# A planner's contention rule, a choice of slots by planned release, and silu behind the second norm's Exp, in a two-layer decoder trunk

## The chip, the cores and the metric

The program runs on one core of a Trainium2 chip. The metric is the device time of one execution in microseconds; of several runs the median counts, and one execution was recorded by the hardware profiler.

## What is computed

Two layers of a decoder trunk on one sequence of 1024 tokens with 1024 channels, all in float32. Each layer has a root-mean-square norm, one input projection, four token mixers of 256 channels, a norm of each mixer's output, an output projection added to the stream, a second norm (`h2` below), and a gated feed-forward network (FFN) added to the stream.

```python
h = rmsnorm(x, attn_norm[l])
c_q, c_kv, k_r, g_b, g_c, u_conv, u_pool, q_sw, k_sw, v_sw = split(h @ w_in[l])
groups = (mla_attention(...), short_gated_conv(...), multiscale_pool(...), swa_sink_attention(...))
mixed = concat(rms_normalised(groups)) * mix_norm[l]
x = x + mixed @ w_o[l]
h2 = rmsnorm(x, ffn_norm[l])
gate, up = split(h2 @ w_gate_up[l])          # 1024 x 2 * 2816
x = x + (silu(gate) * up) @ w_down[l]        # 2816 x 1024
```

A last norm follows the second layer.

## The kernel before

**Products.** Tokens lie along the free axis, in two halves of 512; `HALVES = (1, 0)` says that the second half is worked first. Every large product is made of three matmuls (`mm3`, L260): an operand is split into a high part, which ScalarE casts to fp32r (L280, or L285 with a norm's gain), and a low part, which VectorE makes by subtracting the high part from the operand (L283, or L286 with the gain); high times high, high times low and low times high are added up in PSUM. One matmul has a 128 x 128 weight block and 512 columns.

**Storage.** SBUF is cut into 47 slots of 128 partitions x 1024 numbers, named `u0` to `u46`. `Slots.pair` takes the slot at the head of `places`, a first-in-first-out queue, and `free_pair` puts a slot back at its tail. A new tile in a slot is not written until the last instruction on the tile that it held is through: a wait on whichever engine or transfer that was. The eight PSUM banks (`ps_mm`, `ps_s`, `ps_t`, `ps_pv` and others in the program's names) are given by the planner.

**The start of the FFN.** `out_last` makes the output projection of a token half, adds it to the stream (L1181) and squares the sum (L324). The norm's root comes from `ss2.rnorm(t)`: a matmul with ones sums the squares over the channels (L340, once for the high and once for the low part), ScalarE applies Ln (L349), Exp (L350) and Square (L351), and VectorE makes a Newton step (L352, which reads the matmul's bank last, and L355). Each token half has a root of its own. The products do not wait for the roots: h2 is used without its root, and the root is multiplied into the gate and the up part behind the products (L359, L1454). Silu (L1453, ScalarE) needs another table of functions than Ln and Exp, and a change of table is an instruction of its own (ACT_TABLE_LOAD).

**Gate and up.** The 2816 columns are 22 groups `f` of 128. Group 0 is computed in the plain form, eight products of twelve matmuls (`plain(u)` for half `u`, with `plain_gates` and `plain_acts` behind it). All others use a form with seven products per pair of halves, whose operands are sums of weight blocks and sums of token blocks. Groups 1 and 2 are begun early, among the products of group 0; groups 3 to 21 run in a loop. In the loop GpSimd makes the weight sums (L1213 to L1215, L1243) and the product of silu with the root (L1454); in groups 4 to 19 it also prepares the down-projection's weights: `dn_load` loads two slots of them (L1525), `dn_sum` adds them on GpSimd (L1532) and stores them to DRAM (L1535, the tiles `qd`). The activations' combinations are made on VectorE (L1463) and stored (L1468, the tiles `ad`).

```python
1585        plain(0)
1586        r2.append(F.ap(ss2.rnorm(HALVES[0], tag="pv")))
1587        plain_gates()
1588        combine(0)
1589        plain_acts()
1590        for w in early:
1591            w.split2()
1592        early[0].start()
1593        combine(1)
1594        r2.append(F.ap(ss2.rnorm(HALVES[1], tag="pv")))
1595        plain(1)
```

**What sets the order.** The class `Order` lists every instruction of the traced program with a cost, and schedules them on TensorE, ScalarE, VectorE, GpSimd and SyncE (whose queue issues all DMAs): forward by rank, then backward, in three passes. The order so found is imposed by dependencies without a semaphore. VectorE instructions with two SBUF operands (kind `two`) and GpSimd's TENSOR_TENSOR (kind `pool`) are taken to hinder each other: where they overlap, the VectorE one is made longer by 0.6 of the overlap, up to 1.15 of its own length, and the GpSimd one by 0.6 of it, up to 0.8 us. `scheduled_kernel` repeats this four times, hands the PSUM banks out anew by the planned times each time, and keeps the order with the shortest planned span.

Of the kernel before, what the change touches and what calls it, by code (L numbers as in the profile page):

```python
# [51 lines left out]
class Slots:  # L52
# [59 lines left out]
def trunk_kernel(ctx: ExitStack, tc: tile.TileContext, ins, out, given=None):  # L112
# [10 lines left out]
    slots = Slots(ctx.enter_context(tc.tile_pool(name="slots", bufs=1)), N_U)  # L123
# [174 lines left out]
    class SumSq:  # L298
# [35 lines left out]
        def rnorm(self, t, cols=whole, tag="t", final=None):  # L334
# [15 lines left out]
            act.activation(r0, r0, AF.Exp, scale=-0.5)  # L350
# [67 lines left out]
    for l in range(L):  # L418
# [1032 lines left out]
        def silu(g, r):  # L1451
            nonlocal last_silu
            last_silu = act.activation(g, g, AF.Silu)  # L1453
            pool.tensor_tensor(out=g, in0=g, in1=r, op=ALU.mult)  # L1454
# [123 lines left out]
        plain_acts()  # L1578
# [4 lines left out]
        r2.append(F.ap(ss2.rnorm(HALVES[1], tag="pv")))  # L1583
# [205 lines left out]
        for cols in (slice(0, 256), slice(256, HT)) if last else ():  # L1789
# [11 lines left out]
            finish(x, 1, cols)  # L1801

class Order:
# [7 lines left out]
    SHARED = 0.6  # L1813
# [114 lines left out]
    def run(self, rank, back=False):  # L1928
# [12 lines left out]
        pool = two = 0.0  # L1941
# [9 lines left out]
        for _ in range(self.n):  # L1951
            best = None
            for e in self.ENGINES:
                due(e, free[e])
                if not now[e] and not later[e]:
                    continue
                t = free[e] if now[e] else later[e][0][0]
                if e == "SP" and not back and len(flying) == self.LANES:
                    t = max(t, flying[0])
                if best is None or t < best[0]:  # L1960
                    best = t, e
            t, e = best
            due(e, t)
            k = heapq.heappop(now[e])[1]
            seen, taken = cost[k]
            order[e].append(k)
            if back:
                free[e] = t + taken
                end[k] = -free[e]
            else:  # L1970
                if kind[k] == "two":
# [229 lines left out]
```

## Time and profile before

| | before |
|---|---|
| median of 3 runs | 2063.43 us (2062.45 to 2063.79) |
| profiled execution, its time | 2062.96 us |
| its span in the trace | 2061.2 us |
| granted TensorE clock, mean | 0.998 |
| TensorE busy | 2035.3 us (99%) |
| VectorE / ScalarE / GpSimd busy | 1503.7 / 992.6 / 577.3 us |

The busy time of TensorE counts the matmuls, which are pipelined and whose ends are modelled; the weight loads beside them are listed as PEld. In the rows of the trace DVE is VectorE, ACT ScalarE, POOL GpSimd, SP or SPq the queue that issues the DMAs. A row of the timeline has the start in microseconds, the duration, the engine, the line, the operation, the tiles with their sizes, and in brackets how long the engine had idled and what ended that. A number such as "L283" is a line of the kernel's text. The first layer's FFN begins at about 390 us, the second's at about 1410 us.

### The profile page before, as it was taken

The page shows a single profiled execution, that of the slowest core. Times are in us where ns is not written, and L with a number is a line of the kernel's source. Part 1 is how long each engine was busy: PE and PEld are TensorE (multiplying, and loading weights), DVE is VectorE, ACT ScalarE, POOL GpSimd, SP SyncE. Part 2 cuts the span into 40 slices and gives each one's busy share as a digit, 9 for nine tenths or more (in the row PEclk, how much of TensorE's full clock was granted, in tenths as well). Part 3 has the DMA queues.
Part 4 walks back from the last instruction along what each step waited for, and adds up shares of the span by engine and source line. Part 5 has one row for each costly group of instructions (what it writes and reads, how often), then busy time and mean ns, then how long its engine had stood idle before and what let it go on. Part 6 is the DMA issues. An engine that isn't in the chain of part 4 may idle for free.

```text
span 2061.2 us, 26597 instructions
## 1 busy us (share of the span) xinstructions
PE 2035.3 (99%) x9422; PEld 1673.6 (81%) x9422; DVE 1503.7 (73%) x2443; ACT 992.6 (48%) x1743; POOL 577.3 (28%) x420
## 2 busy tenths in 40 slices
PE   9999999999999999999999999999999999999998
PEld 7887888778888888888888878888788877788887
DVE  8779979987666667655657898889866655585555
ACT  7447657753333334444433666668433333354342
POOL 0200000037777773000002000000577777710000
PEclk9999999999999999999999999999999999999999
DMA  5211223334554556766413112142455555487642
GB/s 191 90 57 46 84 78 96 137 133 168 181 175 167 189 169 235 265 220 208 140 46 124 37 42 97 61 144 94 159 169 178 178 175 170 154 302 237 204 171 96
DMA packets 142118, 302.37 MB, mean 147 GB/s; under 512 B 13856, under 2 KB 60960, under 8 KB 141984
## 3 DMA queue, kind: packets, MB, share of 16 engines
q1 hardware_dynamic: 141984, 300.66, 43.1%
q8 instruction: 74, 1.21, 0.2%
q14 instruction: 60, 0.49, 0.1%
HBM read 212.00 MB, written 87.56 MB: 145 GB/s over the span
## 4 chain that ended last, share of the span: by engine, by line
PE 68%; POOL 7%; DVE 5%; DMA 4%; issue 2%; ACT 2%; SPq 0%; DVEq 0%; POOLq 0%; ACTq 0%
PE ps_mm L260 25%; PE ps_s L260 21%; PE ps_t L260 8%; PE ps_pv L260 6%; POOL u L1532 3%; PE ps_pv L1044 2%; PE ps_t L1032 1%; DMA u<-in_w_dn 1%; POOL tp L1454 1%; DMA ad<-u 1%; POOL u L1214 1%; DVE u L283 1%; POOL u L1213 1%; ACT u L280 1%; DMA u<-in_w_gu 1%
## 5 line engine op out<-in xcount | busy, mean ns | idle before, releaser
L260 PE MATMUL ps_mm<-u,u 128*128 128x512 f32 (+1 forms) x3378 | 831.0, 390 | 3.4 <-ACT u L280 2.3
L260 PEld LDWEIGHTS ps_mm<-u,u 128*128 128x128 f32 x3378 | 615.4, 188 | 130.4 <-issue 5.3
L260 PE MATMUL ps_s<-u,u 128*128 128x512 f32 x2670 | 636.1, 390 | 5.8 <-DVE tn L352 2.3
L283 DVE TENSOR_TENSOR u<-u,u 128x1024 fp32r<-128x1024 f32 (+2 forms) x400 | 443.3, 1126 | 225.2 <-ACT u L280 173.4
L260 PEld LDWEIGHTS ps_s<-u,u 128*128 128x128 f32 x2670 | 499.5, 188 | 117.8 <-ACT tn L1321 3.9
L280 ACT CAST u<-u 128x1024 fp32r<-128x1024 f32 (+2 forms) x400 | 345.1, 881 | 505.4 <-POOL u L1215 60.1
L260 PE MATMUL ps_t<-u,u 128*128 128x512 f32 (+1 forms) x1124 | 255.3, 378 | 2.8 <-DVE u L1447 2.7
L260 PEld LDWEIGHTS ps_t<-u,u 128*128 128x128 f32 x1124 | 201.6, 188 | 45.8 <-DVE u L1447 6.5
L1454 POOL TENSOR_TENSOR tp<-tp,u 128x512 f32<-128x512 f32 x80 | 135.1, 1689 | 341.7 <-ACT tp L1453 341.7
L260 PE MATMUL ps_pv<-u,u 128*128 128x512 f32 x744 | 177.8, 390 | 1.6 <-DVE te L1658 1.0
L260 PEld LDWEIGHTS ps_pv<-u,u 128*128 128x128 f32 x744 | 139.3, 188 | 32.1 <-ACT tn L1321 1.9
L1041 POOL MEMSET u<- 128x128 f32 x32 | 5.9, 211 | 472.9 <-PE ps_pv L1044 149.3
L1453 ACT ACTIVATE tp<-tp 128x512 f32<-128x512 f32 x80 | 50.5, 631 | 155.2 <-DVE tp L359 155.1
L749 POOL TENSOR_TENSOR u<-u,u 128x512 f32<-128x512 f32 x4 | 6.0, 1509 | 380.4 <-PE ps_t L622 288.9
L1532 POOL TENSOR_TENSOR u<-u 128x352 f32<-128x352 f32 x64 | 80.5, 1259 | 31.6 <-DMA u<-in_w_dn 30.2
L280 ACT CAST u<-ps_t 128x512 fp32r<-128x512 f32 (+3 forms) x132 | 65.1, 504 | 48.1 <-PE ps_t L1032 26.7
L1532 POOL TENSOR_TENSOR u<-u,u 128x352 f32<-128x352 f32 x64 | 85.0, 1328 | 3.0
L285 ACT ACTIVATE u<-u,par 128x512 fp32r<-128x512 f32 x100 | 70.6, 717 | 28.5 <-DVE u L359 11.1
L283 DVE TENSOR_TENSOR u<-ps_t,u 128x512 fp32r<-128x512 f32 (+3 forms) x132 | 75.9, 582 | 11.1 <-ACT u L280 9.8
L286 DVE SCALAR_TENSOR_TENSOR u<-u,par,u 128x512 fp32r<-128x512 f32 x100 | 73.7, 750 | 5.9 <-ACT u L285 5.9
L324 ACT ACTIVATE tn<-u 128x512 f32<-128x512 f32 (+1 forms) x91 | 52.3, 595 | 48.6 <-DVE u L1723 42.1
L359 DVE TENSOR_TENSOR tp<-tp,u 128x512 f32<-128x512 f32 x76 | 72.5, 954 | 2.0
(208 smaller groups left out, 2359.3 us busy)
## 6 DMA issues: line engine op xcount, KB each, us to landing
u<-in_w_gu SPq DMA_DIRECT2D x92, 512.0 KB, 4.1
ad<-u SPq DMA_DIRECT2D x154, 256.0 KB, 3.9
u<-ad SPq DMA_DIRECT2D x70, 512.0 KB, 5.1
u<-in_w_dn SPq DMA_DIRECT2D x64, 352.0 KB, 3.4
qd<-u SPq DMA_DIRECT2D x64, 352.0 KB, 2.4
u<-qd SPq DMA_DIRECT2D x32, 512.0 KB, 4.7
u<-in_w_in SPq DMA_DIRECT2D x28, 512.0 KB, 3.5
u<-in_w_dn SPq DMA_DIRECT2D x24, 512.0 KB, 5.2
```

The lines of the kernel that those rows point to most:

```text
L260: pe.matmul(o, w, r, start=start and k == 0 and i == 0, stop=stop and k == n - 1 and i == 2, skip_group_check=again,)
L280: a = act.copy(hi, f)
L283: dve.tensor_tensor(out=lo, in0=f, in1=rd(hi), op=ALU.subtract)
L285: a = act.activation(hi, f, AF.Copy, scale=gain)
L286: dve.scalar_tensor_tensor(out=lo, in0=f, scalar=gain, in1=rd(hi), op0=ALU.mult, op1=ALU.subtract)
L324: act.activation(q, f, AF.Square)
L359: dve.tensor_tensor(out=o, in0=a, in1=b, op=ALU.mult)
L1032: pe.transpose(p[:, b * P : (b + 1) * P], pr[b][j // 4][:, (j % 4) * P : (j % 4 + 1) * P], ident,)
L1044: pe.matmul(py[:, c0:], v_of(j, h), R.ap(s)[:, c0:], start=j == 0 and n == 0, stop=j == nj - 1 and n == 1,)
L1453: last_silu = act.activation(g, g, AF.Silu)
L1454: pool.tensor_tensor(out=g, in0=g, in1=r, op=ALU.mult)
L1532: pool.tensor_tensor(out=o, in0=a, in1=b, op=ALU.add)
```

## The change

Three things are changed. First, the planner's rule for VectorE and GpSimd: instructions of the kinds `two` and `pool` that run at the same time now each get half the speed for as long as they overlap, both without a cap, apart from 0.1 us of each; in the backward pass a `pool` instruction counts 1.3 times its length. Second, `Slots.pair` takes, of the free slots, the one whose last tile is planned to be done with earliest; the planned ends come from the round before. Third, the FFN's start: `silu` of group 0 is called from `plain_acts`, `plain_acts` of the first half stands behind the second root, silu is held behind the second root's Exp by an order without a semaphore, and the second root's matmul goes to a bank of another tag. No arithmetic is added or left out: TensorE has 9394 instructions, VectorE 2445, GpSimd 425 and SyncE 860 in both programs; ScalarE has 1585 before and 1579 after, six table loads fewer.

```diff
-    def __init__(self, pool, n):
+    def __init__(self, pool, n, ends=None):
         self.pool = pool
+        self.ends = iter(ends) if ends else None
+        self.until = [0.0] * n
+        self.asked = []
         self.places = deque(range(n))
         self.halves = {F32: deque(), F32R: deque()}
         self.cur = [None] * n
         self.dt = [None] * n
     def pair(self, dt):
-        i = self.places.popleft()
+        if self.ends:
+            i = min(self.places, key=lambda p: self.until[p])
+            self.places.remove(i)
+            self.until[i] = next(self.ends)
+        else:
+            i = self.places.popleft()
         self.cur[i] = self.pool.tile([P, 2, HT], dt, name=f"u{i}", tag=f"u{i}", bufs=1)
+        self.asked.append(self.cur[i].tensor.name)
...
                 pe.matmul(p, ones, q, start=False, stop=True)
             r0, q = tmp("tn")[:, cols], tmp("tn")[:, cols]
             act.activation(r0, p, AF.Ln, scale=1.0 / n)
-            act.activation(r0, r0, AF.Exp, scale=-0.5)
+            self.exp = act.activation(r0, r0, AF.Exp, scale=-0.5)
             act.activation(q, r0, AF.Square)
             dve.scalar_tensor_tensor(
                 out=q, in0=p, scalar=-0.5 / n, in1=q, op0=ALU.mult, op1=ALU.mult
...
             for f, u, pg, pu in waiting:
                 gate = tmp("tp")
                 mul_to(gate, pg, r2[u])
-                silu(gate, r2[u])
                 gates.append((f, u, gate, pu))
             waiting.clear()
         def plain_acts():
             for f, u, gate, pu in gates:
+                silu(gate, r2[u])
                 acts[f][u] = F.half()
                 mul_to(F.ap(acts[f][u]), pu, gate)
             gates.clear()
...
         def silu(g, r):
             nonlocal last_silu
             last_silu = act.activation(g, g, AF.Silu)
+            behind(last_silu, ss2.exp)
             pool.tensor_tensor(out=g, in0=g, in1=r, op=ALU.mult)
         def combos(g):
...
         r2.append(F.ap(ss2.rnorm(HALVES[0], tag="pv")))
         plain_gates()
         combine(0)
-        plain_acts()
         for w in early:
             w.split2()
         early[0].start()
         combine(1)
-        r2.append(F.ap(ss2.rnorm(HALVES[1], tag="pv")))
+        r2.append(F.ap(ss2.rnorm(HALVES[1], tag="t")))
+        plain_acts()
         plain(1)
         early[1].start()
         combine(2)
...
-    SHARED = 0.6
+    SHARED = 1.3
+    LEAST = 0.1
...
-                if kind[k] == "two":
-                    more = min(max(0.0, min(pool, t + 2 * seen) - t) * self.SHARED, 1.15 * seen)
-                    seen, taken = seen + more, taken + more
-                    two = t + seen
-                elif kind[k] == "pool":
-                    more = min(0.8, max(0.0, two - t) * self.SHARED)
-                    seen, taken = seen + more, taken + more
-                    pool = t + seen
...
+        def on(t):
+            nonlocal clock
+            if t > clock:
+                for x in sharing.values():
+                    x[1] -= (t - clock) / len(sharing)
+                clock = t
...
+            if sharing:
+                t, e = min((clock + max(x[1], 0.0) * len(sharing), e) for e, x in sharing.items())
+                if best is None or t <= best[0]:
+                    on(t)
+                    k, _, began = sharing.pop(e)
+                    end[k] = t + self.LEAST
+                    free[e] = end[k] - cost[k][0] + cost[k][1]
+                    release(k, began)
+                    continue
...
+            if back:
+                free[e] = t + taken * (self.SHARED if kind[k] == "pool" else 1.0)
+                end[k] = -free[e]
+            elif kind[k] in ("two", "pool"):
+                on(t)
+                sharing[e] = [k, seen - self.LEAST, t]
...
+    def ends(self, end, asked):
+
+
+
+        return [max((end[k] for k in self.users[m]), default=0.0) for m in asked]
...
+        given = plan.banks(end), plan.ends(end, asked)
+        nc, traced, asked = trace(*given)
         plan = Order(traced, nc.dependency_edges)
-        found = plan.find()
-        if best is None or found[0] < best[0]:
-            best = found[0], banks, found[1]
-    return trace(best[1], best[2])[0]
+        span, order, end = plan.find()
+        if best is None or span < best[0]:
+            best = span, given, order
```

The planner's new rules change the order on all engines. Three places are shown, all in the first layer. The numbers behind a tile's name count the tiles; the slot is the number right behind `u`. A line's number after the change is 9 or 10 higher than before (L280 is L289, L283 is L292, L349 is L358, L1202 is L1211).

The first place is the second root of the FFN. ScalarE before, with Ln (L349), Exp (L350) and Square (L351) of the second root; silu of group 0 (L1453) stands further ahead:

```order
L349 ACT_TABLE_LOAD
L349 ACTIVATE tn_4232<-ps_pv_4229 128x512
L280 CAST u4_4218<-tp_4209 128x512
L350 ACT_TABLE_LOAD
L350 ACTIVATE tn_4232<-tn_4232 128x512
L280 CAST u32_4215<-tp_4210 128x512
L280 CAST u39_4222<-tp_4211 128x512
L1142 ACTIVATE te_4319<-u31_2542,par_75 128x512
L351 ACTIVATE tn_4233<-tn_4232 128x512
```

ScalarE after, with Ln (L358), Exp (L359) and Square (L360) of the same root and silu of group 0 (L1462):

```order
L358 ACTIVATE tn_4229<-ps_t_4226 128x512
L289 CAST u16_2213<-tp_4146 128x512
L359 ACTIVATE tn_4229<-tn_4229 128x512
L1462 ACT_TABLE_LOAD
L1462 ACTIVATE tp_4139<-tp_4139 128x512
L289 CAST u25_4157<-tp_4147 128x512
L1151 ACTIVATE te_4202<-u8_3957,par_75 128x512
L360 ACTIVATE tn_4230<-tn_4229 128x512
```

No table load stands among the root's steps now but the one for silu, and silu has moved behind Exp. On TensorE the root's two matmuls (L340) stood here before, among the products of group 0 and of the early groups:

```order
L260 MATMUL ps_t_4239<-u43_4069,u9_3933 128x512
L260 MATMUL ps_t_4176<-u20_3824,u33_4167 128x512 x2
L260 MATMUL ps_t_4176<-u20_3824,u46_4168 128x512
L260 MATMUL ps_t_4176<-u15_3854,u33_4167 128x512 x2
L260 MATMUL ps_t_4176<-u15_3854,u46_4168 128x512
L340 MATMUL ps_pv_4229<-u44_4076,ones_r_79 128x512 x2
L260 MATMUL ps_t_4176<-u25_3884,u33_4167 128x512 x2
```

and after the change they are L349:

```order
L269 MATMUL ps_s_4080<-u23_3914,u41_3928 128x512 x2
L269 MATMUL ps_s_4080<-u23_3914,u29_3929 128x512
L349 MATMUL ps_t_4226<-u22_4076,ones_r_79 128x512 x2
L269 MATMUL ps_s_4240<-u17_2225,u9_3932 128x512
L269 MATMUL ps_s_4172<-u39_3811,u38_3946 128x512 x2
L269 MATMUL ps_s_4172<-u39_3811,u1_3947 128x512
```

They are now TensorE's instructions 1895 and 1896; before they were 1936 and 1937. In the second layer they move by three places. The tile `u_4076` is the split sum of squares of the second half.

The second place is the beginning of group 3. VectorE before, with the addition of two products (L1658, tile `te_4670`), the weights' low parts (L283) and the combinations of the activations (L1463):

```order
L283 TENSOR_TENSOR u12_4638<-u17_4561,u22_4637 128x1024
L283 TENSOR_TENSOR u40_4620<-u6_4560,u11_4619 128x1024
L1463 TENSOR_TENSOR u35_4420<-u46_4551,u35_4420 128x512
L283 TENSOR_TENSOR u6_4673<-u27_4568,u10_4672 128x1024
L1658 TENSOR_TENSOR te_4670<-ps_pv_4587,tn_4654 128x512
```

VectorE after, where L1658 is L1668 and L1463 is L1473:

```order
L292 TENSOR_TENSOR u14_4620<-u10_4559,u2_4619 128x1024
L292 TENSOR_TENSOR u34_4638<-u38_4560,u41_4637 128x1024
L1668 TENSOR_TENSOR te_4670<-ps_pv_4587,tn_4654 128x512
L292 TENSOR_TENSOR u13_4673<-u12_4567,u11_4672 128x1024
L1680 TENSOR_TENSOR tp_4689<-ps_mm_4641,tn_4635 128x512
L1473 TENSOR_TENSOR u15_2542<-u15_2542,u33_3186 128x512
```

The addition has moved ahead of the combination and of one of the low parts. The third place is the queue of DMAs in group 9, with the loads of a later group's weights (L1202 and L1204, tiles `u_6048` and `u_6049`), the loads and stores of the down-projection's weights (L1525, L1535) and a store of activations (L1624). Before:

```order
L1202 DMA u35_6048<-in_w_gu 128x1024
L1535 DMA qd2_97<-u40_5950 128x2x352
L1535 DMA qd2_97<-u18_5949 128x2x352
L1525 DMA u31_6091<-in_w_dn 128x2x352
L1525 DMA u6_6092<-in_w_dn 128x2x352
L1204 DMA u18_6049<-in_w_gu 128x1024
L1624 DMA ad0_88<-u7_3957 128x512
L1535 DMA qd2_97<-u6_6092 128x2x352
```

After:

```order
L1211 DMA u41_6048<-in_w_gu 128x1024
L1213 DMA u34_6049<-in_w_gu 128x1024
L1545 DMA qd2_97<-u12_5950 128x2x352
L1535 DMA u24_6091<-in_w_dn 128x2x352
L1535 DMA u12_6092<-in_w_dn 128x2x352
L1634 DMA ad0_88<-u8_3957 128x512
L1545 DMA qd2_97<-u5_5949 128x2x352
L1545 DMA qd2_97<-u12_6092 128x2x352
```

The second load of the weights now stands ahead of the stores and goes to slot 34; before it went to slot 18, which the second of those stores reads. In the same way the high part of tile `u_5895` was cast into slot 40 before (`u40_6087`, the slot of the sums in `u40_5950`) and is cast into slot 26 after (`u26_6087`, the slot of a raw weight tile whose last split is earlier). From the loop's groups to the down-projection the order on TensorE itself is the same before and after; in the mixers and at the FFN's start it differs.

More of the change, by code (lines that the diff above doesn't have):

```diff
@@ L111, in trunk_kernel @@
 @with_exitstack
-def trunk_kernel(ctx: ExitStack, tc: tile.TileContext, ins, out, given=None):
+def trunk_kernel(ctx: ExitStack, tc: tile.TileContext, ins, out, given=None, ends=None):
     nc = tc.nc
@@ L1801, in trunk_kernel @@
             finish(x, 1, cols)
+    return slots.asked
 class Order:
@@ L1940, in run @@
         flying, served = deque(), 0.0
-        pool = two = 0.0
+        sharing, clock = {}, 0.0
         for k in range(self.n):
@@ L1949, in due, with release @@
                 heapq.heappush(now[e], (rank[k], k))
[L1951 to L1970, printed above, removed]
[L1971 to L1986 removed]
+        def on(t):
[4 more added lines that the diff above has]
+                clock = t
+        def release(k, t):
+            e = self.engine[k]
             for j, sync in ahead[k]:
```

62 lines of the change are left out of this document (42 added, 20 removed).

## The prediction

> **What bounds the kernel now.** I read the page first, for the engine that fills the span; then the windows of TensorE, to find in which stages it loses time; then the waits of TensorE; then the timeline around each wait. The page's row of busy times, and a table of windows (from and to, length, TensorE busy and matmuls, granted clock, DMA share, GB/s):
>
> ```profile
> PE 2035.3 (99%) x9422; PEld 1673.6 (81%) x9422; DVE 1503.7 (73%) x2443; ACT 992.6 (48%) x1743; POOL 577.3 (28%) x420
> ...
> 396.00:480.00 84.00, 79.90 (x348) 1.00 0.34 117
> 640.00:815.00 175.00, 173.09 (x756) 1.00 0.55 183
> 820.00:1010.00 190.00, 190.00 (x840) 1.00 0.67 225
> 1420.00:1500.00 80.00, 77.19 (x338) 1.00 0.37 127
> 1500.00:1640.00 140.00, 139.74 (x615) 1.00 0.51 173
> 1640.00:1830.00 190.00, 187.72 (x813) 1.00 0.55 180
> ```
>
> TensorE bounds the kernel: only 26 us of 2061.2 are not busy. The change removes no matmul, so all it can win is time in which TensorE waits or is fed late. The fourth window lies in the first layer's down-projection: 840 matmuls in 190.00 us, with no gap, 0.2262 us each. Other windows of these stages have the same kind of matmul, so what each lost is its length less its matmuls times 0.2262: 5.3 and 3.5 us in the two starts of the FFN (first and fifth window), 4.0, 0.9 and 6.1 us in the later gate and up groups (the others). That is 8.8 us and 11.0 us for the two layers together. The down-projection has nothing to win.
>
> The waits of TensorE (what waits, what for; us in total, times, longest):
>
> ```profile
> PE ps_t L260 <- DVE u L1447: 2.7, 7, 1.2
> PE ps_s L260 <- DVE tn L352: 2.3, 1, 2.3
> PE ps_mm L260 <- ACT u L280: 2.3, 2, 1.5
> ...
> PE ps_pv L260 <- DVE te L1658: 1.0, 1, 1.0
> PE ps_s L260 <- DVE te L1658: 1.0, 1, 1.0
> ...
> PE ps_pv L634 <- DVE u L283: 0.8, 1, 0.8
> PE ps_s L260 <- DVE u L1181: 0.7, 1, 0.7
> PE ps_pv L260 <- ACT tn L1321: 0.6, 1, 0.6
> ```
>
> The first row is the loop over the groups; the next four are the FFN's starts, 6.6 us of their 8.8; the last three lie in the mixers and the output projection.
>
> **The second root.** The timeline of the first layer, from the sum of squares (L326) and its low part (L283, 404.39) over the root's matmul to the product that waits for the bank:
>
> ```profile
> 399.53 0.70 DVE L326 SCALAR_TENSOR_TENSOR u<-tn,u 128x512 f32<-128x512 f32 x1
> ...
> 404.39 0.70 DVE L283 TENSOR_TENSOR u<-u,u 128x512 fp32r<-128x512 f32 x1
> ...
> 408.86 0.62 PE L340 MATMUL ps_pv<-u,ones_r 128*128 128x512 f32 x2
> ...
> 411.27 1.28 ACT L349 ACT_TABLE_LOAD   x1
> 412.56 0.60 ACT L349 ACTIVATE tn<-ps_pv 128x512 f32<-128x512 f32 x1
> ...
> 413.69 1.28 ACT L350 ACT_TABLE_LOAD   x1
> ...
> 418.61 0.68 DVE L352 SCALAR_TENSOR_TENSOR tn<-ps_pv,tn 128x512 f32<-128x512 f32 x1
> 419.35 0.97 PE L260 MATMUL ps_s<-u,u 128*128 128x512 f32 x3 [2.34 <-DVE tn L352]
> ```
>
> From the matmul's end at 409.5 to L352's end at 419.3 the chain takes 9.8 us, two table loads of 1.28 among them. After the change one load stands in it, silu's, between Exp and Square: 1.28 us less, but silu itself stands there too. What removes the stall is the place of the matmul, 41 matmuls or 41 x 0.2262 = 9.3 us earlier: the bank comes free several us ahead of its next use, and 2.3 us go.
>
> [...]
>
> The price is a new wait. Earlier by 9.3 us, the matmul comes due at 399.6. Its low part was made at 405.1, and the four low parts with a gain that stood ahead of L326 are now spread behind. L326 still has to follow the last square, and one low part with a gain and one wide low part stand between it and the tile: 399.53 + 0.70 + 0.76 + 1.24 + 0.70 = 402.9 if L326 does not gain, 400.5 if it gains the 2.4 us by which its square was done before it:
>
> ```profile
> 396.47 0.63 ACT L324 ACTIVATE tn<-u 128x512 f32<-128x512 f32 x1
> 400.73 0.76 DVE L286 SCALAR_TENSOR_TENSOR u<-u,par,u 128x512 fp32r<-128x512 f32 x1
> 401.99 1.24 DVE L283 TENSOR_TENSOR u<-u,u 128x1024 fp32r<-128x1024 f32 x1
> ```
>
> So TensorE waits 0.9 to 3.3 us here; I take 2.0, nearly the middle, and keep 0 (if other matmuls slip ahead in time as well) and 5.5 (if the tile is as late as before) for the range. In the second layer the matmul moves by three places, 0.7 us, and I count nothing.
>
> **Silu's place.** In both layers a product waited for a cast behind silu's table load:
>
> ```profile
> 426.77 1.28 ACT L1453 ACT_TABLE_LOAD   x1
> ...
> 429.68 2.56 PE L260 MATMUL ps_mm<-u,u 128*128 128x512 f32 x10 [0.73 <-ACT u L280]
> ```
>
> With all first-group silus behind the second root, Exp and silu alternate no more and this load is gone. The 2.3 us of the third wait row go in the two layers; the cast here can come 1.28 us sooner, for a wait of 0.73. Silu's product on GpSimd and the first half's activation come later, and that is free: the combinations that read them are made at group 3 (465.60 below).
>
> **The start of group 3.** Two products waited for L1658, once in each layer. VectorE and TensorE in the first:
>
> ```profile
> 465.60 1.77 DVE L1463 TENSOR_TENSOR u<-u,u 128x512 f32<-128x512 f32 x1
> 467.29 2.31 DVE L283 TENSOR_TENSOR u<-u,u 128x1024 fp32r<-128x1024 f32 x1
> 469.53 0.68 DVE L1658 TENSOR_TENSOR te<-ps_pv,tn 128x512 f32<-128x512 f32 x1
> 470.26 3.03 PE L260 MATMUL ps_pv<-u,u 128*128 128x512 f32 x12 [0.96 <-DVE te L1658]
> ```
>
> L1463 and one low part stand behind L1658 now, 4.0 us of work for a wait of 0.96. The low part that comes later is needed by a later product; I count 1.4 of the 2.0 us as won and leave 0.6 for it. The FFN's starts: 2.3 + 2.3 + 1.4 - 2.0 = 4.0 us won.
>
> **The groups.** In the loop the stall repeats in odd groups. A cast of the next group's weights, the low part behind it, L1447 behind that in VectorE's queue, and the product that wants L1447's bank:
>
> ```profile
> 644.66 1.06 ACT L280 CAST u<-u 128x1024 fp32r<-128x1024 f32 x1 [4.24 <-POOL u L1532]
> 684.07 1.05 ACT L280 CAST u<-u 128x1024 fp32r<-128x1024 f32 x1 [4.58 <-DMA qd<-u]
> 685.16 1.78 DVE L283 TENSOR_TENSOR u<-u,u 128x1024 fp32r<-128x1024 f32 x1 [2.25 <-ACT u L280]
> 685.82 2.25 POOL L1215 TENSOR_TENSOR u<-u,u 128x512 f32<-128x512 f32 x1
> ...
> 687.60 2.79 PE L260 MATMUL ps_t<-u,u 128*128 128x512 f32 x11 [1.17 <-DVE u L1447]
> ```
>
> The cast does not lack its operand. It waits for the slot it writes to: the first-in-first-out queue gave it the slot of the down-projection's sums, whose last GpSimd sum or store is late. In the new order such casts get slots of weights split long before (slot 26 instead of 40), and the loads of weights stand ahead of the stores in SyncE's queue. A cast that may start some 4 us earlier takes the low part and L1447 out of TensorE's way. What is late next: other casts now get the sums' slots, and every load that waits for a slot holds the queue behind it. Those casts have some us until their low parts are read, by the order, but their starts depend on GpSimd. So of the 11.0 us I count 6 as won; the bounds are 10, if all casts are free, and -4, if another such wait appears beside each that goes.
>
> **The mixers.** Their order changes on all engines and nothing there is aimed at a stall. The three mixer rows sum to 2.1 us. I count 1 us lost, with -2 (those waits gone) and +4 (two more sets of them) as the bounds of the cost. The four passes over weights in the down-projection keep TensorE's order: nothing.
>
> **The sum.** -6 - 4 + 1 = -9 on the profiled execution's 2062.96 us: 2053.96. The median of the runs is 0.47 above that execution, so 2054.4 us.
>
> **Rivals.** The first: the new rule is not what the chip does, so the plan's times, on which both orders and slots hang, are off by as much as the old ones.
>
> ```profile
> 440.50 2.37 DVE L283 TENSOR_TENSOR u<-u,u 128x1024 fp32r<-128x1024 f32 x1 [0.40 <-ACT u L280]
> 440.50 1.28 POOL L1213 TENSOR_TENSOR u<-u,u 128x512 f32<-128x512 f32 x1
> 446.66 1.23 DVE L283 TENSOR_TENSOR u<-u,u 128x1024 fp32r<-128x1024 f32 x1
> ```
>
> GpSimd took its 1.28 us unhindered, and VectorE took 1.23 (its time alone, third row) and 1.14 more, nearly all of GpSimd's time. Half speed each would have had both at about 2.4. So the one that is first runs through and the other stands still. [...] A VectorE step of 1.23 that meets a GpSimd step of 2.25 then ends up to 2.25 + 1.23 = 3.5 us after its start, where half speed plans 2.5: 1.0 us off, the size of the stall at 687.60. If that eats the groups' gain, the sum is 0 - 4 + 1 = -3: 2060.4 us, which is within 0.2% (4.1 us, about what a measurement of this kernel can tell from no change). Against it: the total of both steps is right by either rule, and slots, not contention, hold the casts that stall now. Chance 0.2.
>
> The second rival ends slower: slots by planned release bring the cast's wait into every group. The slot with the earliest planned end is chosen by times that assume half speed; where GpSimd's sums run later, casts and loads wait in more groups, and each waiting load holds SyncE's queue. Groups 4 to 19 of two layers are 32; 7 stall now by the first wait row, for 11.0 us, 1.6 each. With 7 more stalls and none of the old ones gone the sum is 11 - 4 + 1 = +8: 2071 us. It decides from 7 us of new stalls on, five groups, since the 3 us won elsewhere and the 4.1 us of the bound come first. For it speak 4.24 and 4.58 us of idleness before the casts above; against it, that the new order holds those waits at casts needed later. Chance 0.15.
>
> **How the numbers follow.** The forecast has 0.65. With the groups and the mixers at their good ends (-10 and -2), and no wait ahead of the root's matmul (-6), the sum is -18: 2045.4. With half of the groups' gain (-3), 5.5 us ahead of the root's matmul (-0.5) and +4 in the mixers it is +0.5, 2063.9. Neither is likely in all its parts at once. To hold eight in ten I take 2046 to 2066, which has the first rival in it and ends between it and the second. Faster by over 0.2%: nearly all of the forecast, a little of the first rival, 0.64. Within 0.2%: most of the first rival and the forecast's upper edge, 0.19. Slower: the second rival and some mishap in the mixers, 0.17.
>
> **What would show it.** Right: no table load of L358 or L359 in the FFN's start, the product behind the second root's bank not waiting, at most 3 us of waiting ahead of the root's matmul, TensorE's waits for L1456 (L1447 before) below 1.5 us in all, casts in odd groups that idle for their load and not for GpSimd or a store, and windows of the groups that lose under 5 us together. Wrong: casts that wait over 4 us for sums or stores in even groups too, a TensorE wait of 4 us or more at the second root, or more than 6 us of waits in the mixers.

## The result and the profile after

The changed kernel takes 2063.96 us (median of 13 runs, 2062.37 to 2068.96); the kernel before took 2063.78 us in the 13 runs beside it. The ratio is 1.0005, with a 95% interval of 0.9997 to 1.0014: no change that can be measured. Forecast were 2054.4 us, 0.4% faster. The profiled execution of the changed kernel took 2065.5 us, its span is 2063.7 us against 2061.2 before.

TensorE's waits in the changed kernel (line waited for, us in total, times, longest):

```profile
PE ps_t L631 <- DVE tp L620: 8.2, 8, 2.0
PE ps_t L269 <- DVE u L1456: 5.5, 6, 1.0
...
PE ps_s L269 <- DVE u L292: 1.0, 1, 1.0
PE ps_mm L269 <- ACT u L289: 0.9, 1, 0.9
```

The waits that stood at the FFN's starts are gone: none for the second root (L352 before, L361 now), none for casts where there were 2.3 (the 0.9 for L289 lies at 6.4 us, at the program's start), none for L1668 (L1658 before). Two smaller ones are new there, 1.0 for L292 in the first layer and 0.5 for L368 in the second. The first row is new and larger than all of them. L631 transposes the probabilities of the window attention, and L620 is the VectorE step that scales them. TensorE's windows after, at the places shown of before:

```profile
396.00:480.00 84.00, 82.71 (x363) 1.00 0.32 110
480.00:640.00 160.00, 158.98 (x701) 1.00 0.53 182
640.00:815.00 175.00, 173.19 (x763) 1.00 0.52 177
...
1420.00:1500.00 80.00, 79.50 (x347) 1.00 0.34 117
1500.00:1640.00 140.00, 139.11 (x614) 1.00 0.54 180
1640.00:1830.00 190.00, 188.18 (x830) 1.00 0.51 176
```

By the prediction's count (length less 0.2262 us for each matmul) the two starts lose 1.9 and 1.5 us, where they lost 5.3 and 3.5; the groups lose 1.4, 2.4, 1.1 and 2.3, 7.2 us in all against 11.0. So some 9 us were won in the FFN, where 10 were forecast, and given back in the mixers.

A second count has no windows to choose. TensorE has the same number of instructions in all the kernels here, so the start of its n-th instruction can be compared between two traces, and the difference grows or shrinks stage by stage. The stages end, in both layers alike, at the 1800th instruction of the layer (before the FFN's start), the 2400th (behind group 3) and the 3900th (in the down-projection). In us, changed less before: mixers +3.6 and +7.1, FFN's starts -2.3 and -2.1, groups -0.05 and -3.6; before rounding they sum to +2.5, the difference of the spans.

**Where the mixers lost it.** GpSimd makes sums of the early groups' weights (L758 to L761, L749 to L752 before) ahead of the FFN, in the middle of the mixers. In the kernel before, the first of them starts at 91.7 us; in the changed kernel it starts at 76.1, beside the softmax of the window attention. The timeline of the changed kernel, GpSimd, VectorE and TensorE:

```profile
76.13 1.29 POOL L758 TENSOR_TENSOR u<-u,u 128x512 f32<-128x512 f32 x1 [75.69 <-DMA u<-in_w_gu]
77.38 2.26 POOL L759 TENSOR_TENSOR u<-u,u 128x512 f32<-128x512 f32 x1
79.71 1.26 POOL L760 TENSOR_TENSOR u<-u,u 128x512 f32<-128x512 f32 x1
81.05 1.27 POOL L761 TENSOR_TENSOR u<-u 128x512 f32<-128x512 f32 x1
...
78.42 1.23 DVE L615 TENSOR_TENSOR sm<-sm,par 128x2 f32<-128x2 f32 x1
...
80.05 2.43 DVE L620 TENSOR_SCALAR tp<-tp,sm 128x256 f32<-128x256 f32 x2
...
81.27 0.30 PE L631 MATMUL ps_t<-cst,tp 128*128 128x128 f32 x1 [1.99 <-DVE tp L620]
82.53 0.78 PE L631 MATMUL ps_t<-cst,tp 128*128 128x128 f32 x3 [0.72 <-DVE tp L620]
```

The same pair of scalings in the kernel before took a quarter of that, and its two-column addition (L606 there) about a ninth; the first sums follow later. Their row merges the two sets and names, of the several transfers that they wait for, the one that landed last:

```profile
77.49 0.14 DVE L606 TENSOR_TENSOR sm<-sm,par 128x2 f32<-128x2 f32 x1
...
77.95 0.61 DVE L611 TENSOR_SCALAR tp<-tp,sm 128x256 f32<-128x256 f32 x2
...
91.75 2.72 POOL L749 TENSOR_TENSOR u<-u,u 128x512 f32<-128x512 f32 x2 [91.30 <-DMA vraw<-in_w_ukv]
```

L615 ends when the GpSimd sum beside it ends (77.38 + 2.26 = 79.64). The two scalings end shortly after one sum each (the sums at 80.97 and 82.32); the second ends at 82.48. Four such sets of sums, two in each layer, give the eight waits.

### The profile page after: what moved, and what is told of

The parts are those of the page before. It is cut to its first block, busy times and chain, and to the rows that moved or that the text cites. A ratio compares the mean times of both kernels' runs of the same rounds, so it can differ in the third digit from the quotient of the medians.

```text
span 2063.7 us, 26584 instructions
## 1 busy us (share of the span) xinstructions
PE 2033.8 (99%) x9422; PEld 1675.0 (81%) x9422; DVE 1563.2 (76%) x2443; ACT 988.9 (48%) x1737; POOL 575.6 (28%) x420
## 4 chain that ended last, share of the span: by engine, by line
PE 86%; DVE 7%; ACT 3%; issue 2%; DMA 1%; POOL 0%; SPq 0%; DVEq 0%; ACTq 0%; POOLq 0%
PE ps_mm L269 33%; PE ps_s L269 27%; PE ps_t L269 10%; PE ps_pv L269 8%; PE ps_pv L1053 2%; PE ps_t L1041 1%; DVE u L292 1%; DVE u L295 1%; PE ps_s L987 1%; PE ps_s L988 1%; PE ps_s L989 1%; DMA u<-in_w_gu 1%; ACT u L294 1%; PE ps_pv L643 1%; PE ps_t L631 1%
## 5 line engine op out<-in xcount | busy, mean ns | idle before, releaser
L292 DVE TENSOR_TENSOR u<-u,u 128x1024 fp32r<-128x1024 f32 (+2 forms) x400 | 461.0, 1173 | 185.7 <-ACT u L289 124.7
L289 ACT CAST u<-u 128x1024 fp32r<-128x1024 f32 (+2 forms) x400 | 344.9, 881 | 450.4 <-DVE u L292 81.5
L1462 ACT ACTIVATE tp<-tp 128x512 f32<-128x512 f32 x80 | 50.6, 632 | 138.4 <-DVE tp L368 138.2
L758 POOL TENSOR_TENSOR u<-u,u 128x512 f32<-128x512 f32 x4 | 6.2, 1558 | 362.7 <-DVE sm L617 271.1
L289 ACT CAST u<-ps_t 128x512 fp32r<-128x512 f32 (+3 forms) x132 | 64.9, 503 | 50.5 <-PE ps_t L1041 25.6
L1542 POOL TENSOR_TENSOR u<-u,u 128x352 f32<-128x352 f32 x64 | 82.7, 1292 | 2.1
L1542 POOL TENSOR_TENSOR u<-u 128x352 f32<-128x352 f32 x64 | 76.5, 1196 | 21.1 <-DMA u<-in_w_dn 21.1
L292 DVE TENSOR_TENSOR u<-ps_t,u 128x512 fp32r<-128x512 f32 (+3 forms) x132 | 75.5, 581 | 8.7 <-ACT u L289 7.1
L368 DVE TENSOR_TENSOR tp<-tp,u 128x512 f32<-128x512 f32 x76 | 77.6, 1021 | 1.4
```

The source lines that it names most:

```text
L289: a = act.copy(hi, f)
L292: dve.tensor_tensor(out=lo, in0=f, in1=rd(hi), op=ALU.subtract)
L368: dve.tensor_tensor(out=o, in0=a, in1=b, op=ALU.mult)
L1542: pool.tensor_tensor(out=o, in0=a, in1=b, op=ALU.add)
```

## The experiments

Port theory: the sums moved beside the softmax and hold VectorE up there, in the way of the prediction's first rival: the step that is first runs through and the other stands still. The runs can show the holding up; a port as such is visible in none of them. Order theory, its rival: the new order and slots lose time in the mixers in many places, and the sums only lie there. Stage differences are taken from each kernel's profiled execution against that of before, as above (both layers together); each ratio is to runs of the kernel before on the same chip. Plan and queue are the two ways to choose a slot:

| kernel | rule | slots | FFN's start | median, us | ratio to before, 95% interval | mixers | starts | groups |
|---|---|---|---|---|---|---|---|---|
| changed | new | plan | new | 2063.96 | 1.0005 (0.9997 to 1.0014) | +10.7 | -4.5 | -3.7 |
| a_sums_light | new | plan | new | 2054.31 | 0.9947 (0.9934 to 0.9959) | -1.0 | -4.2 | -3.4 |
| b_sums_light | old | queue | old | 2063.43 | 0.9998 (0.9989 to 1.0007) | +0.6 | +1.5 | -0.4 |
| a_dn_light | new | plan | new | 2058.33 | 0.9966 (0.9954 to 0.9979) | +5.9 | -4.5 | -11.1 |
| a_kinds | new | plan | new | 2062.09 | 0.9986 (0.9977 to 0.9994) | +9.4 | -4.5 | -3.4 |
| a_hold | new | plan | new | 2054.65 | 0.9957 (0.9943 to 0.9971) | -1.2 | -4.1 | -3.2 |
| a_fifo | new | queue | new | 2046.18 | 0.9913 (0.9900 to 0.9927) | -2.6 | -4.2 | -11.2 |
| a_fifo_hold | new | queue | new | 2046.37 | 0.9915 (0.9902 to 0.9929) | -3.1 | -1.2 | -10.9 |
| a_old_rule | old | plan | new | 2060.93 | 0.9985 (0.9976 to 0.9994) | +7.3 | -2.8 | -9.1 |
| a_old_hold | old | plan | new | 2049.91 | 0.9933 (0.9919 to 0.9946) | -1.7 | -2.9 | -8.5 |
| b_slots | old | plan | old | 2069.97 | 1.0028 (1.0015 to 1.0042) | +11.1 | +4.3 | -7.9 |
| b_rule | new | queue | old | 2050.64 | 0.9939 (0.9927 to 0.9952) | -3.4 | +1.3 | -10.2 |
| b_silu | old | queue | new | 2066.11 | 1.0009 (1.0000 to 1.0017) | -2.1 | +0.9 | +3.5 |

The changed kernel and a_dn_light have the same order in the mixers and differ there by almost 5 us in one execution each, so that column is good to some microseconds; a_dn_light's profiled execution was also the fastest of its six (2053.28). The medians carry the verdicts.

**Without the sums, in the same order.** In `a_sums_light` the plan is that of the changed kernel, and only in the program built from it (`final`) the four sums become memsets:

```diff
-            pool.tensor_tensor(out=F.ap(q + 1), in0=a21, in1=a22, op=ALU.add)
-            pool.tensor_tensor(out=F.ap(q), in0=a21, in1=a11, op=ALU.add)
-            pool.tensor_tensor(out=a21, in0=F.ap(q + 1), in1=a11, op=ALU.add)
-            pool.tensor_tensor(out=a12, in0=a12, in1=a21, op=ALU.add)
+            if final:
+                for o in (F.ap(q + 1), F.ap(q), a21, a12):
+                    pool.memset(o, 0.0)
+            else:
...
```

> The changed kernel in its own order, slots and banks, in which only the four GpSimd sums of the early groups' weights (L758 to L761, two sets in each layer) are replaced by memsets of the same tiles, so the weights of groups 1 and 2 are left out. Port theory: the mixers lose time because these sums run beside the softmax of the window attention and hold VectorE's scalings (L620) and its two-column steps (L615, L617). Then L620 falls from 455 ns to about 350, TensorE's wait for it from 8.2 us to under 1.5, and the time by 6 to 10 us, to about 2056. Order theory: the mixers' loss comes from the new order and slots in general, and the sums only happen to lie there: the waits of TensorE in the mixers stay above 5 us in all and the time falls by less than 3.

Measured: 2054.31 us, some 10 us less than the changed kernel. The group of the scalings before, in the changed kernel, and in this one (busy, mean ns of one):

```profile
L611 DVE TENSOR_SCALAR tp<-tp,sm 128x256 f32<-128x256 f32 (+1 forms) x64 | 20.0, 348 | 0.5
```

```profile
L620 DVE TENSOR_SCALAR tp<-tp,sm 128x256 f32<-128x256 f32 (+1 forms) x64 | 27.2, 455 | 0.4
```

```profile
L620 DVE TENSOR_SCALAR tp<-tp,sm 128x256 f32<-128x256 f32 (+1 forms) x64 | 19.7, 339 | 0.4
```

No wait of TensorE for L620 is left in the list; the first row is the groups' (the line numbers are 4 higher there):

```profile
PE ps_t L269 <- DVE u L1460: 5.7, 6, 1.0
```

The port theory's numbers came; the order theory's did not. Of the 11.7 us between the two kernels' mixers (+10.7 and -1.0), 8.2 are the waits for L620, and about 2 are a lower clock behind the first of them (0.91 from 80 to 100 us in the changed kernel, last section). The same memsets in the kernel before, as a control:

> The kernel before in its own order, with the same memsets in place of the same sums (the weights of groups 1 and 2 are left out). Port theory: the sums lie beside other work there (two-operand steps of the pooling mixer), so taking them away gains 0 to 2 us: 2062 to 2064. If they cost as much there as in the changed kernel (6 to 10 us), the change did not bring the loss by moving them, and the port theory falls.

Measured: 2063.43 us, a ratio of 0.9998 (0.9989 to 1.0007). Where they were, the sums cost nothing that can be measured.

**The sums held back.** `a_hold` does all the work; the two sums that stand first in each set wait by a semaphore for the scaling of the eighth attention unit, and the planner knows of it.

```diff
-            pool.tensor_tensor(out=F.ap(q + 1), in0=a21, in1=a22, op=ALU.add)
-            pool.tensor_tensor(out=F.ap(q), in0=a21, in1=a11, op=ALU.add)
+            for o, a in ((F.ap(q + 1), a22), (F.ap(q), a11)):
+                tc.add_manual_dep(
+                    pool.tensor_tensor(out=o, in0=a21, in1=a, op=ALU.add).ins,
+                    scaled[0].ins.name,
+                    mybir.DependencyInfo(mybir.DependencyClass.Sync, mybir.DependencyReason.DATA),
+                    reason="hold",
+                )
```

> The changed kernel in which GpSimd's sums for the early groups may start only when VectorE has done the scaling (L620) of the eighth unit of the window attention, by a semaphore; the planner knows of it and plans anew; all work is done. Port theory: from there to the ninth unit there is no scaling, so L620 averages under 370 ns, TensorE waits under 1.5 us for it, and the 10 us that the memsets gave come back nearly whole: 2054 to 2058. Order theory: with another order and the sums later, slots are freed later and loads queue: 2060 to 2066.

Measured: 2054.65 us. The scalings (L621 here) are back at their own length:

```profile
L621 DVE TENSOR_SCALAR tp<-tp,sm 128x256 f32<-128x256 f32 (+1 forms) x64 | 19.4, 338 | 0.2
```

Two other plans got the same semaphore: one whose sums lie late anyway (a control), and one with the old rule, whose sums lie early.

> New rule, first-in-first-out slots, silu's new place, and the semaphore that keeps the early groups' sums behind the eighth unit's scaling. A control for the semaphore: in this kernel without it the sums lie behind that scaling anyway (92 to 102 us). Port theory: the semaphore finds nothing to mend, 2044 to 2049 as without it. If holding helps by the other order that it draws, this one gains by several us too: under 2042.

> Old rule, slots by plan, silu's new place, and the semaphore. Port theory: L620 falls from 426 to under 370 ns, TensorE's 8.6 us of waits for it to under 1.5, and the time by 7 to 10 us from 2061: 2051 to 2054. Order theory: 2057 or more.

Measured: 2046.37 us against 2046.18 without it, and 2049.91 against 2060.93. The semaphore gains 9 to 11 us where sums lie beside the softmax and nothing where they do not. The last time is 1 us under the range I gave; the two medians come from two chips, and against the kernel before on each the gain is about 10.

**Which edit moved the sums.** The three edits apart. `a_fifo` gives the slots by the queue again.

```diff
-            asked = trunk_kernel(tc, ins, out, banks, ends)
+            asked = trunk_kernel(tc, ins, out, banks)
```

> The changed kernel with the first-in-first-out choice of slots put back (new contention rule and silu's place kept). If the choice of slots brought the sums' loads forward (their slots wait for TensorE alone instead of for later readers), the sums move back behind the softmax: L620 under 380 ns, mixers lose under 4 us, but the waits of casts for slots come back in the groups (L1456, 2.5 to 5 us in windows that lose some 10 us): 2057 to 2062. If the new rule moved them, L620 stays near 450 ns, and the time is 2063 to 2070.

Measured: 2046.18 us, far below either expectation and, with `a_fifo_hold`, the fastest of all. The sums start late again; GpSimd, first and last of the two sets in the first layer:

```profile
90.33 1.72 POOL L758 TENSOR_TENSOR u<-u,u 128x512 f32<-128x512 f32 x1 [89.89 <-DMA u<-in_w_gu]
...
100.53 1.62 POOL L761 TENSOR_TENSOR u<-u 128x512 f32<-128x512 f32 x1
```

And the groups' stalls, which I expected to return, are gone from its windows:

```profile
640.00:815.00 175.00, 175.00 (x773) 1.00 0.60 200
...
1640.00:1830.00 190.00, 190.00 (x840) 1.00 0.60 199
```

`a_old_rule` has the old planner's loop and its 0.6:

```diff
-    SHARED = 1.3
-    LEAST = 0.1
+    SHARED = 0.6
...
+                if kind[k] == "two":
+                    more = min(max(0.0, min(pool, t + 2 * seen) - t) * self.SHARED, 1.15 * seen)
```

> The changed kernel with the old contention rule put back (slots by plan and silu's place kept). If the choice of slots moved the sums, L620 stays near 450 ns, TensorE waits over 5 us for it, and the time is 2062 to 2067. If the new rule moved them, L620 is near 350 ns and the time 2052 to 2058.

Measured: 2060.93 us, 1 us under the first expectation's range, with L620 at 426 ns. TensorE waits for L620 under the old rule too:

```profile
PE ps_t L631 <- DVE tp L620: 8.6, 8, 2.2
```

`b_slots` is the kernel before with the slots by plan alone, `b_rule` with the rule alone; both undo the edits at the FFN's start, as here (from `b_rule`) for silu and the second root:

```diff
-            behind(last_silu, ss2.exp)
...
-        r2.append(F.ap(ss2.rnorm(HALVES[1], tag="t")))
-        plain_acts()
+        r2.append(F.ap(ss2.rnorm(HALVES[1], tag="pv")))
```

> The kernel before with the choice of slots by plan alone. If that choice brings the sums' loads forward under any rule: L620 over 420 ns and over 5 us of TensorE's waits for it, a loss of 6 to 9 us in the mixers. If it frees the groups' casts from slots as the forecast said: casts idle under 10 us in all for GpSimd's sums and stores in the two windows (47 before) and the windows of the groups lose under 4 us instead of 11. The time then is 2061 to 2066.

> The kernel before with the new contention rule alone: first-in-first-out slots, the FFN's start as it was. If the rule is what gained the 18 us of the run with first-in-first-out slots: 2046 to 2050, and what it lacks against 2046 is what the edits at the FFN's start are worth under this rule (forecast 4 us, 1 or nothing by the run that had them alone). If the three edits only work together: over 2055.

Measured: 2069.97 us, slower than expected, with 8.3 us of waits for L620; and 2050.64 us, 0.6 over the range. So the choice of slots moves the sums, whichever rule stands beside it. With slots by plan the first sum starts at 75.7 to 77.6 us (the changed kernel, a_kinds, a_old_rule, b_slots), with the queue at 90.3 to 91.7 (before, a_fifo, b_rule, b_silu). In the first layer the first sum starts when its operands have landed: in the changed kernel (76.13 us) and in a_fifo (90.33) the rows above name a load of `in_w_gu` as what ended GpSimd's idle time, and these loads landed 3.4 to 4.3 us after their issue in the changed kernel, 3.4 to 4.8 in the one before. Each of the two sets in a layer has two loads (L747 before, L756 after). The queue's kernel (here the one before) and then the changed kernel issue those of the first layer so:

```profile
47.59 0.33 SPq L747 DMA_DIRECT2D u<-in_w_gu  x1
...
71.73 0.33 SPq L747 DMA_DIRECT2D u<-in_w_gu  x1
...
85.19 1.98 SPq L747 DMA_DIRECT2D u<-in_w_gu  x2
```

```profile
71.29 7.60 SPq L756 DMA_DIRECT2D u<-in_w_gu  x3
...
87.12 0.33 SPq L756 DMA_DIRECT2D u<-in_w_gu  x1
```

Not all loads come earlier: the first of the queue's kernel goes out 24 us ahead of any in the changed kernel. By the tiles' numbers in the two programs, the loads at 47.59 and 71.73 belong to the set that is summed second, and the set that is summed first waits for the two from 85.19 on. In the changed kernel the two loads of the first set are the first that go out.

`b_silu` makes those edits alone, in the kernel before:

```diff
+            behind(last_silu, ss2.exp)
...
-        r2.append(F.ap(ss2.rnorm(HALVES[1], tag="pv")))
+        r2.append(F.ap(ss2.rnorm(HALVES[1], tag="t")))
+        plain_acts()
```

> The kernel before with only the edits at the FFN's start: silu behind the second root's Exp, called later, and the other bank; old rule, first-in-first-out slots. My forecast's term for the FFN's starts (2.3 for the bank, 2.3 for the casts behind silu's table load) then holds by itself: these windows lose 4 to 6 us instead of 8.8, six table loads are gone, and the time falls by 3 to 5 us, to about 2060. Rival: the starts were mended by the planner's rule (the place of L1668), and this edit alone gives less than 2 us: 2062 to 2064.

Measured: 2066.11 us, a ratio of 1.0009 with an interval from 1.0000: neither expectation's gain. Six table loads are gone (two silu loads are left of the eight that stood there), but TensorE waits for other steps at the starts, 1.7 and 1.4 us for L1333. Under the new rule the same edits are worth 4 us (b_rule less a_fifo, 2050.64 to 2046.18), under slots by plan and the old rule 9 (b_slots less a_old_rule), each taken across two chips. What they win hangs on the plan that is drawn around them; the runs do not say why the old plan with the queue gains nothing.

**Telling the planner.** `a_kinds` counts the scalings and the two-column additions as steps that share with GpSimd.

```diff
+        if e == "DVE" and len(aps) == 1 and op == "TensorScalarPtr" and not i.is_scalar_tensor_tensor:
+            return None if aps[0].memref.startswith("ps_") else "two"
+        small = [a.memref for a in i.ins if hasattr(a, "memref")]
+        if e == "DVE" and op == "TensorTensor" and len(small) == 2 and not aps:
+            return "two"
```

> The changed kernel, with one addition to the planner: VectorE's scalings with one SBUF operand (L620) and the two-column additions (L615, L617) count as steps that share with GpSimd. Everything is planned anew. Port theory: the plan then sees what the sums cost beside the softmax and puts them elsewhere; L620 averages under 380 ns, TensorE waits under 3 us for it, and the time is 2053 to 2060. Order theory: a new order is drawn and the time lies anywhere within 4 us of 2064, whatever L620 does.

Measured: 2062.09 us, and TensorE still waits for L620:

```profile
PE ps_t L631 <- DVE tp L620: 6.1, 8, 1.6
```

The port theory's expectation failed: the sums start at 77.6 us and are not put elsewhere. The time lies where the order theory had put it, but with the sums in their old place the run cannot decide between the two. A likely reason, argued from the code and not tested: the planner starts whatever is ready on an idle engine, so a price can lengthen the sums but not postpone them.

**What is left in the groups.** In the changed kernel a stall at 611 us, VectorE, GpSimd and TensorE:

```profile
605.83 1.56 DVE L292 TENSOR_TENSOR u<-u,u 128x512 fp32r<-128x512 f32 x1
607.32 1.44 DVE L368 TENSOR_TENSOR tp<-tp,u 128x512 f32<-128x512 f32 x1
608.68 2.31 DVE L292 TENSOR_TENSOR u<-u,u 128x1024 fp32r<-128x1024 f32 x1
...
606.79 1.41 POOL L1542 TENSOR_TENSOR u<-u 128x352 f32<-128x352 f32 x1
608.16 1.74 POOL L1224 TENSOR_TENSOR u<-u,u 128x512 f32<-128x512 f32 x1
609.87 2.25 POOL L1464 TENSOR_TENSOR tp<-tp,u 128x512 f32<-128x512 f32 x1
...
611.65 1.65 PE L269 MATMUL ps_t<-u,u 128*128 128x512 f32 x6 [1.02 <-DVE u L1456]
```

Three VectorE steps in a row take 5.3 us together; a low part of 1024 columns alone took 1.23 before. In `a_dn_light` the down-projection's sums (L1542) become memsets in the changed kernel's order, again only in the program built from the plan:

```diff
-                pool.tensor_tensor(out=o, in0=a, in1=b, op=ALU.add)
+                if final:
+                    pool.memset(o, 0.0)
+                else:
...
```

> The changed kernel in its own order, with the GpSimd sums of the down-projection's weights (L1542, groups 4 to 19) replaced by memsets, so these sums are left out. Contention theory: the waits for L1456 that are left in the groups (5.5 us, 6 times) come from VectorE's low parts stretched beside GpSimd's sums, no longer from casts that wait for slots: they fall below 1.5 us, and the time by 4 to 7 us, to about 2059. Slot theory: those waits come from casts behind a slot or a load, and at least 3 us of them stay; the time falls by less than 3.

Measured: 2058.33 us, about 6 us under the changed kernel; the waits for L1456 are gone and the windows full:

```profile
640.00:815.00 175.00, 175.00 (x773) 1.00 0.57 189
...
1640.00:1830.00 190.00, 190.00 (x840) 1.00 0.58 192
```

So the stalls that the changed kernel keeps come from GpSimd's sums. A memset is also through sooner with its slot (0.39 us on the average from 560 to 815 us, where the two forms of the changed kernel's sums took 1.33 and 1.09), but slots are not what stalls: casts still wait for the stores of these slots in this run, more than in the changed kernel, while TensorE loses nothing. ScalarE's wait from 560 to 815 us in `a_dn_light`:

```profile
ACT u L289 <- DMA qd<-u: 12.8, 3, 4.7
```

What is left is what the timeline shows, VectorE's steps stretched beside the sums. In the changed kernel the casts' waits for the sums' slots are indeed nearly gone; instead casts wait for low parts (L292, 30.3 us, where the same wait for L283 was 0.7 before). The same stretch, before and then after:

```profile
ACT u L280 <- POOL u L1532: 18.5, 5, 4.3
...
ACT u L280 <- DMA qd<-u: 4.6, 1, 4.6
```

```profile
ACT u L289 <- DVE u L292: 30.3, 11, 4.1
...
ACT u L289 <- POOL u L1542: 3.3, 1, 3.3
```

Slots by plan under the old rule leave no such wait there (b_slots) and win 7.9 us in the groups; the new rule with the queue wins 10.2 (b_rule). Either alone clears most of the loss, and the two together leave two thirds of it. Why they get in each other's way is open.

**The better version.** `a_fifo`, the change without its choice of slots, is faster than both kernels: 2046.18 us, 0.9913 of before (0.9900 to 0.9927).

## Why the prediction was wrong

- **The FFN's starts: right.** Forecast -4, found -4.5. The bank's wait is gone, and the chain is shorter where it was said to be:

```profile
404.21 0.62 PE L349 MATMUL ps_t<-u,ones_r 128*128 128x512 f32 x2
...
408.33 0.60 ACT L358 ACTIVATE tn<-ps_t 128x512 f32<-128x512 f32 x1
409.33 0.64 ACT L359 ACTIVATE tn<-tn 128x512 f32<-128x512 f32 x1
410.00 1.28 ACT L1462 ACT_TABLE_LOAD   x1
...
417.50 0.67 DVE L361 SCALAR_TENSOR_TENSOR tn<-ps_t,tn 128x512 f32<-128x512 f32 x1
```

  The chain took more time than before (404.8 to 418.2, 13.3 us against 9.8), and nobody waited, since the matmul stands earlier in the order; the place did it, not the table load. The 2.0 us of waiting ahead of the early matmul did not come: it follows the product before it without a gap. In its place stand two new waits of 1.5 us together (L292, L368), which no term had; that the sum fits so well is in part luck. That the edits there do this by themselves is refuted by b_silu.
- **The groups: direction right, size off.** Forecast -6, found -3.7. The casts' waits show that casts were freed from the sums' slots; that this is what won the 3.7 us is not shown, since in `a_dn_light` casts wait for those slots and nothing stalls. What took the rest was named only as a chance of other casts waiting; it is VectorE beside GpSimd's sums (a_dn_light). My reason for giving contention little weight there, that slots hold the casts that stall, is refuted as the whole story by a_fifo and b_rule: with the queue's slots and the new rule the stalls vanish.
- **The mixers: the step that failed.** The prediction said "Their order changes on all engines and nothing there is aimed at a stall", took 1 us lost, and bounded it by -2 and +4. Found: +10.7, with 8.2 us of waits for L620, a wait that did not exist before; over 6 us of waits in the mixers was the prediction's own sign of being wrong. The bounds came from the waits that stood there, and a new wait is not bounded by the old ones. I followed the new slots in the groups and never asked which loads they would start earlier elsewhere, though the loads of the early groups' weights stand in the same queue.
- **The rivals.** The first had the right mechanism, one engine runs through and the other stands still (L615 beside L759 ended 0.01 us after it), but priced it in the groups and between steps that the plan counts. The cost fell on steps that the plan does not count at all. The rows that the prediction showed for it are of a VectorE step with two operands in SBUF (L283); L620, with one SBUF tensor, went from 348 to 455 ns on the average, and was at 339 without the sums (a_sums_light). The second rival, waits in every group, did not happen.
- **The range** held the time, because it had been drawn up to 2066 to take in the first rival's 2060.4; the forecast, faster, did not hold. That is luck: none of the sums behind the range has 10 us lost in the mixers.

## What to carry to other kernels

When a planner hands out buffers by another rule, look at every load whose start it moves, at which loads then come together, and at what they set off, above all work on GpSimd beside short VectorE chains that TensorE waits for. Bound a reordered stage by what its tightest chain would lose beside a neighbour that it does not have yet, not by the waits that it has. And take a bundle of edits apart before judging it: here two of three were worth 18 us, and the third took them back.

## What the runs showed of the hardware

A VectorE addition of two columns that met a GpSimd sum lasted until the sum ended: L615 took 1.23 us beside L759, where the 28 of its 32 executions that meet no sum took 0.14 to 0.17 in the same trace. All four that met one ended within 0.02 us of the sum's end. The time of these four was not the step's size but the neighbour's.

Behind the waits the clock was lower in some executions. After the 1.99 and 0.72 us of waiting the granted clock of TensorE (the column behind the brackets) fell to half, for some 3.4 us by these rows (they lack 0.33, 0.50 and 0.03 of the full clock in 2 us each, 1.7 us in all, which is 3.4 us at half), in the profiled execution of the changed kernel:

```profile
80.00:82.00 2.00, 0.54 (x2) 1.00 0.94 356
82.00:84.00 2.00, 1.47 (x6) 0.67 0.33 131
84.00:86.00 2.00, 2.00 (x7) 0.50 0.00 0
86.00:88.00 2.00, 2.00 (x11) 0.97 0.00 0
```

From 80 to 100 us the clock averaged 0.91 in the changed kernel, in a_kinds and in b_slots, and 1.00 in a_dn_light and a_old_rule, which wait there too (TensorE was busy 16.1, 16.5 and 16.0 us of the 20 in the first three, 17.5 and 17.3 in the other two): about 2 us that some of these executions lose and others do not. The two waits ahead of the drop are 2.7 us in all; what decides whether a wait is followed by one, no run here shows.
